# Recurrence products in column groups: the diagonal and four-block levels of a hybrid decoder trunk

## The chip, the cores and the metric

One core of a Trainium2 chip runs the whole kernel. The metric is the device time of one execution in microseconds (us), the median of several runs; a run that is profiled gives a trace as well. The engines are named as the profile names them: PE is TensorE (PEld its weight loads), DVE is VectorE, ACT is ScalarE, POOL is GpSimd, SP is SyncE, which issues the DMAs here.

## The reference

Two layers of a decoder trunk on 256 tokens of width 2048. In each layer a shared input projection feeds attention and, beside it, a gated linear recurrence of 8 heads (HGRN2) with 128 key and 128 value columns a head. Then come an output projection, a gated feed-forward part, and a gated input embedding. The change is in the recurrence alone:

```python
def hgrn2_chunkwise(q, k, v, log_f):
    ...
    def step(state, inp):
        q_, k_, v_, g_ = inp
        b = jnp.cumsum(g_, axis=2)
        diff = b[:, :, :, None, :] - b[:, :, None, :, :]
        decay = jnp.exp(jnp.where(causal[None, None, :, :, None], diff, MASK_VALUE))
        a = jnp.einsum('bhtk,bhsk,bhtsk->bhts', q_, k_, decay)
        o = jnp.einsum('bhts,bhsv->bhtv', a, v_) + \
            jnp.einsum('bhtk,bhkv->bhtv', q_ * jnp.exp(b), state)
```

So the score of a query token t against an earlier token s is a sum over the 128 key columns of q, k and the product of the forget gates between s and t.

## The kernel before

**Projections.** Nearly all of the time goes to large projections. Weights come by DMA in pieces of 256 rows and 512 columns (512 KB), 10 buffers (`wr`). ACT makes a rounded copy of each (`wh`, L305) and DVE the remainder (`wl`, L315), 7 buffers each. `strip` (L330, L331, L333) multiplies a piece by the two 128-token halves: three matmuls of 512 columns for each half and 128 rows, twelve a piece. After each piece `tick()` advances the work that runs beside the projections: generators and delayed functions. These emit their instructions between the projection's.

**Order.** The kernel is written with a tile framework. It finds the dependencies, and its scheduler lays out the order of each engine's instructions when the program is built; on the chip each engine keeps that order. `behind("pe")` holds an instruction behind the projection matmul emitted last. Accesses to one bank of PSUM (where TensorE writes its results) are kept apart: a read of a bank by DVE or ACT and a write to it by TensorE do not overlap. The small products share four banks (`bank()`, tag `ms`).

**The recurrence.** `Rec` handles four heads at once, and there are two groups a layer, so four `Rec` in all. Each runs beside the projections of its own gates (`done_f`, `done_q`, `done_i`, `done_g`). It holds q, k and the gates transposed (128 key columns in the partitions, tokens along the free axis) and fills the score tile `s.at` (source token s in the partitions, target t along the free axis, two halves of 128 tokens, four heads). It does so level by level, from small blocks of tokens to large ones:

- diagonal (`levels`, L1046): a token with itself and with its neighbour. For each half and head one product of k's 128 tokens (stationary) with `s.qd` (128 plain columns and 64 odd ones that carry one gate). DVE takes the diagonal by a multiplication with the identity (L1049) and the neighbours by a masked copy (L1051).
- four-block levels for blocks of 2 and of 8 tokens (`four`, L1009): one product for each half and head of k's 128 tokens with 192 columns of `s.qf`, then three masked copies (L1018) for every two heads. Between them `up`, `prepare` and `up_four` (L977 to L1038) multiply the gates into q, k and f on DVE and build the next `s.qf` (ACT L994, DVE L995 and L997).
- levels of 32 and 64 (L1075): only the blocks needed, 32 or 64 stationary columns, each block's result in its own partitions, copied by ACT (L1077).
- then the block between the two halves (L1082) and the products with v (L1101, L1102).

In the diagonal and four-block levels all 128 source tokens are multiplied with all columns, and only blocks within 32 tokens of the diagonal are kept. `s.at` is written whole by L1049, which puts zeros outside the diagonal. Each of these levels takes eight products, two to a bank, four banks.

Of the kernel before, what the change touches and what calls it, by code (L numbers as in the profile page):

```python
# [8 lines left out]
F32 = mybir.dt.float32  # L9
F32R = mybir.dt.float32r  # L10
I32 = mybir.dt.int32
AF = mybir.ActivationFunctionType
ALU = mybir.AluOpType
AX = mybir.AxisListType

P = 128
SEQ = 256
NT = 2
D = 2048
# [28 lines left out]
def decoder(ctx: ExitStack, tc: tile.TileContext, x, p, positions, w_in, attn_sinks,  # L48
# [9 lines left out]
    sp = ctx.enter_context(tc.tile_pool(name="sp", bufs=1))  # L58
# [6 lines left out]
    V, S, G, T = nc.vector, nc.scalar, nc.gpsimd, nc.tensor  # L65
# [41 lines left out]
    def bank(shape=(P, W)):  # L107
        return pms.tile(list(shape), F32, tag="ms", name="ms")
# [29 lines left out]
    ident = cp.tile([P, P], F32, name="ident")  # L138
# [22 lines left out]
    at = 0  # L161
    for g in (pre_ffn_gain, ple_gain, attn_out_gain, hgrn_out_gain):
        n = DEPTH * g.shape[1] // P
# [429 lines left out]
    m_one = cp.tile([P, 64], F32, name="m_one")  # L593
    m_four = cp.tile([P, 2, 192], F32, name="m_four")
# [155 lines left out]
    for l in range(DEPTH):  # L750
# [45 lines left out]
        def done_q(half):  # L796
            qT[half] = sp.tile([P, 4, SEQ], F32, tag="AB"[half], name="qT")

            def done(t, ps):
                tb = tables(t)  # L800
                o = nat()
                ov = o.rearrange("p (g two j d) -> p g j two d", j=4, g=2, two=2)
                rotate(ps, tb, 0, 8, ov[:, :, :, 0], ov[:, :, :, 1])
                start(attend(half, t, o))
            return done
# [107 lines left out]
        class Rec:  # L913


            def __init__(s, grp):
                s.grp = grp
                s.has_v = set()
                s.f = sp.tile([P, 4, SEQ], F32, tag="A", name="f")
                s.k = sp.tile([P, 4, SEQ], F32, tag="B", name="k")  # L920
                s.q = sp.tile([P, 4, SEQ], F32, tag="C", name="q")
                s.at = sp.tile([P, NT, 4, P], F32, tag="at", name="at")
                s.ax = sp.tile([P, 4, P], F32, tag="ax", name="ax")

            def done_f(s, t, ps):
                z = nat()
                S.activation(z, ps, AF.Copy, scale=rx(t)[:, 0:1])


                def turn():  # L930
                    pt = bank((P, 4, P))
                    for b in range(4):
                        T.transpose(pt[:, b], z[:, b * P:(b + 1) * P], ident)
                    cols = slice(t * P, (t + 1) * P)
                    S.activation(s.f[:, :, cols], pt, AF.Sigmoid)
                    S.activation(s.k[:, :, cols], pt, AF.Sigmoid, scale=-1.0)
                    for h in range(4):
                        c = s.grp * 4 + h
                        V.tensor_scalar(s.f[:, h, cols], s.f[:, h, cols], omlb[:, l, c:c + 1],
                                        lb[:, l, c:c + 1], op0=ALU.mult, op1=ALU.add)  # L940
                        V.tensor_scalar(s.k[:, h, cols], s.k[:, h, cols], omlb[:, l, c:c + 1],
                                        None, op0=ALU.mult)
                later(5, turn)

            def done_q(s, t, ps):
                sg = nat()
                S.activation(sg, ps, AF.Sigmoid, scale=rx(t)[:, 0:1])
                V.scalar_tensor_tensor(sg, ps, rx(t)[:, 0:1], sg, op0=ALU.mult, op1=ALU.mult)

                if t == 0:  # L950
                    s.qd = sp.tile([P, 4, NT, P + 64], F32, tag="D", name="qd")

                def turn():
                    pt = bank((P, 4, P))
                    for b in range(4):
                        T.transpose(pt[:, b], sg[:, b * P:(b + 1) * P], ident)
                    raw = s.qd[:, :, t, 0:P]
                    cols = slice(t * P, (t + 1) * P)
                    S.copy(raw, pt)

                    def odd(a):
                        return a.rearrange("p h (b two) -> p h b two", two=2)[:, :, :, 1]
                    V.tensor_tensor(s.qd[:, :, t, P:P + 64], odd(raw), odd(s.f[:, :, cols]),
                                    op=ALU.mult)
                    V.tensor_tensor(s.q[:, :, cols], raw, s.f[:, :, cols], op=ALU.mult)
                    if t == 1:
                        start(s.levels())
                later(3 - t, turn)
# [30 lines left out]

            def four(s, k):  # L1000

                for t in range(NT):
                    for h0 in (0, 2):
                        pl = bank((P, 2, 192))
                        for g in range(2):
                            h = h0 + g
                            c = h * 64 + t * 32
                            with behind("pe"):
                                T.matmul(pl[:, g].rearrange("p (b six k) -> p b six k", six=6, k=k),  # L1009
                                         s.k[:, h, t * P:(t + 1) * P],  # L1010
                                         s.qf[:, :, c:c + 32].rearrange("p v (b k) -> p b v k", k=k),
                                         start=True, stop=True)
                        at = s.at[:, t, h0:h0 + 2].rearrange("p g (b m) -> p g b m", m=4 * k)
                        pv = pl.rearrange("p g (b m) -> p g b m", m=6 * k)
                        mv = m_four[:, (2, 8).index(k)].rearrange("p (b m) -> p b m", m=6 * k)
                        for v0, n in ((0, 3), (3, 2), (5, 1)):
                            cols = slice(v0 * k, (v0 + n) * k)
                            V.copy_predicated(  # L1018
                                at[:, :, :, (4 - n) * k:4 * k],
                                mv[:, :, cols].bitcast(I32).unsqueeze(1)  # L1020
                                .to_broadcast([P, 2, 32 // k, n * k]),
                                pv[:, :, :, cols])

            def up_four(s, k):
                qv, kv, fv, qf = s.views(k)
# [13 lines left out]

            def levels(s):  # L1040
                yield
                for t in range(NT):
                    for h0 in (0, 2):
                        pd = bank((P, 2, P + 64))
                        for h in range(2):
                            T.matmul(pd[:, h], s.k[:, h0 + h, t * P:(t + 1) * P],  # L1046
                                     s.qd[:, h0 + h, t], start=True, stop=True)
                        at = s.at[:, t, h0:h0 + 2]
                        V.tensor_tensor(at, pd[:, :, 0:P],  # L1049
                                        ident.unsqueeze(1).to_broadcast([P, 2, P]), op=ALU.mult)  # L1050
                        V.copy_predicated(  # L1051
                            at.rearrange("p h (b two) -> p h b two", two=2)[:, :, :, 1],
                            m_one.bitcast(I32).unsqueeze(1).to_broadcast([P, 2, 64]),
                            pd[:, :, P:P + 64])
                s.up(1)
                s.prepare(2)
                yield
                yield
                yield
                s.four(2)  # L1060
                s.up_four(2)
                s.prepare(8)
                yield
                yield
                s.four(8)
                s.up_four(8)
                yield
                for k in (32, 64):
                    pl = bank((P, NT, 4, k))
                    for s0 in range(0, P, 2 * k):  # L1070
                        rows = slice(s0, s0 + k)
                        for t in range(NT):
                            for h in range(4):
                                c = t * P + s0
                                T.matmul(pl[rows, t, h], s.k[:, h, c:c + k],  # L1075
                                         s.q[:, h, c + k:c + 2 * k], start=True, stop=True)
                        S.copy(s.at[rows, :, :, s0 + k:s0 + 2 * k], pl[rows])  # L1077
                    s.up(k)
                    yield
                px = bank((P, 4, P))  # L1080
                for h in range(4):
                    T.matmul(px[:, h], s.k[:, h, 0:P], s.q[:, h, P:2 * P], start=True, stop=True)  # L1082
                S.copy(s.ax, px)
                yield
                for t in range(NT):
                    while t not in s.has_v:
                        yield
                    s.out(t)
# [119 lines left out]
        for gi, glen in enumerate(FF_GROUPS):  # L1208
# [3 lines left out]
            while len(hidden) < want:  # L1212
                n = len(hidden)
# [121 lines left out]
```

## Time and profile before

| | |
|---|---|
| median of 3 runs | 2378.17 us |
| lowest and highest | 2377.51, 2379.47 us |
| the profiled execution | 2380.66 us |
| its span, first to last instruction | 2378.9 us |
| granted TensorE clock | 0.998 |

A row of the groups gives line, engine, operation, tiles (out<-in), for TensorE the weights' size, the shapes, the count, then after the bar the busy time in us and the mean ns of one, and the idle time before them. A row of the timeline gives start and length in us, then the same, with the count of instructions merged into it and, in brackets, how long the engine stood idle before and what ended that. Matmuls overlap in a pipeline, so the length of one is more than its share of the time; the distance between starts is the share.

### The profile page before, as it was taken

Reading aid. Unit: us, or ns where it says so; the run is one execution under the profiler, and the core shown is the slowest. Engines: PE = TensorE matmul, PEld = TensorE weight load, DVE = VectorE, ACT = ScalarE, POOL = GpSimd, SP = SyncE. Lnnn points to the kernel's source line nnn. Section 1 sums busy time; section 2 is a strip of 40 time slices with the busy share of each in tenths; the row PEclk is TensorE's granted clock in tenths of the full one; section 3 lists DMA queues with packets and bytes.
Section 4 is the critical chain, followed back from the end, with each engine's and each line's share of the span. In section 5 each row is a group of like instructions: output and inputs, shape, how many; then the busy total and the mean of one; then the engine's idle time right before and its main releaser. Section 6 shows DMA issues by size and latency. Waiting matters only on the chain.

```text
span 2378.9 us, 31721 instructions
## 1 busy us (share of the span) xinstructions
PE 2358.3 (99%) x10951; PEld 1950.6 (82%) x10951; DVE 2026.5 (85%) x2703; ACT 1398.0 (59%) x2000; POOL 106.6 (4%) x213
## 2 busy tenths in 40 slices
PE   9999999999999999999999999999999999999999
PEld 7888887887888888888788888878878888888887
DVE  7687987999999899888777879779999989998885
ACT  6565466556556555657556554665566565565564
POOL 3100001000000000001010000010000000000010
PEclk9999999999999999999999999999999999999999
DMA  8666467657566664766776663675765575667753
GB/s 290 216 187 203 151 199 250 223 199 244 181 226 219 241 230 166 272 220 203 227 222 207 184 209 132 226 257 180 241 219 193 206 254 198 230 209 251 243 169 133
DMA packets 301666, 506.05 MB, mean 213 GB/s; under 512 B 23712, under 2 KB 69696, under 8 KB 301504
## 3 DMA queue, kind: packets, MB, share of 16 engines
q1 hardware_dynamic: 301200, 503.93, 63.6%
q8 instruction: 86, 1.41, 0.2%
q14 instruction: 76, 0.62, 0.1%
q10 hardware_dynamic: 240, 0.07, 0.0%
q0 software_dynamic: 64, 0.02, 0.0%
HBM read 474.57 MB, written 29.36 MB: 212 GB/s over the span
## 4 chain that ended last, share of the span: by engine, by line
PE 92%; DVE 4%; issue 1%; DMA 1%; ACT 1%; POOL 1%; SPq 0%; DVEq 0%; ACTq 0%; POOLq 0%
PE acc L331 9%; PE acc L330 9%; PE acc L333 9%; PE accc L418 5%; PE accc L421 5%; PE accc L422 5%; PE acca L422 4%; PE acce L422 4%; PE acce L418 4%; PE acca L418 4%; PE acca L421 4%; PE acce L421 4%; PE accd L422 3%; PE accd L418 3%; PE accd L421 3%; PE ms L418 3%
## 5 line engine op out<-in xcount | busy, mean ns | idle before, releaser
L305 ACT CAST wh<-wr 128x1024 fp32r<-128x1024 f32 x980 | 1006.0, 1051 | 722.9 <-DVE wr L434 209.3
L315 DVE TENSOR_TENSOR wl<-wr,wh 128x1024 fp32r<-128x1024 f32 x980 | 1163.0, 1217 | 212.7 <-ACT wh L305 204.9
L330 PE MATMUL acc<-wh,ck 128*128 128x512 f32 x1056 | 417.5, 396 | 0.8 <-ACT ck L203 0.8
L331 PE MATMUL acc<-wh,ck 128*128 128x512 f32 x1056 | 413.4, 392 | 0.0
L333 PE MATMUL acc<-wl,ck 128*128 128x512 f32 x1056 | 412.2, 391 | 0.8 <-DVE wl L315 0.8
L434 DVE TENSOR_TENSOR wr<-wr 128x1024 f32<-128x1024 f32 (+1 forms) x240 | 243.8, 1038 | 0.8
L333 PEld LDWEIGHTS acc<-wl,ck 128*128 128x128 f32 x1056 | 198.7, 188 | 43.0 <-DVE wl L315 1.7
L331 PEld LDWEIGHTS acc<-wh,ck 128*128 128x128 f32 x1056 | 198.9, 188 | 40.3 <-DVE ck L204 0.4
L330 PEld LDWEIGHTS acc<-wh,ck 128*128 128x128 f32 x1056 | 198.5, 188 | 40.6 <-ACT ck L203 1.0
L418 PE MATMUL acca<-wh,ck 128*128 128x512 f32 x468 | 182.6, 390 | 3.1 <-ACT wh L305 3.1
L422 PE MATMUL acca<-wl,ck 128*128 128x512 f32 x468 | 182.3, 390 | 1.1 <-DVE wl L315 1.1
L418 PE MATMUL acce<-wh,ck 128*128 128x512 f32 x468 | 182.7, 390 | 0.4 <-ACT wh L305 0.4
L422 PE MATMUL acce<-wl,ck 128*128 128x512 f32 x468 | 182.3, 390 | 0.3 <-DVE wl L315 0.2
L421 PE MATMUL acce<-wh,ck 128*128 128x512 f32 x468 | 182.1, 389 | 0.0
L421 PE MATMUL acca<-wh,ck 128*128 128x512 f32 x468 | 182.1, 389 | 0.0
L422 PE MATMUL accd<-wl,ck 128*128 128x512 f32 x368 | 144.7, 393 | 0.0
L418 PE MATMUL accd<-wh,ck 128*128 128x512 f32 x368 | 143.7, 390 | 0.0
L421 PE MATMUL accd<-wh,ck 128*128 128x512 f32 x368 | 143.2, 389 | 0.0
L421 PE MATMUL accc<-wh,ck 128*128 128x512 f32 x368 | 143.2, 389 | 0.0
L422 PE MATMUL accc<-wl,ck 128*128 128x512 f32 x368 | 143.2, 389 | 0.0
L418 PE MATMUL accc<-wh,ck 128*128 128x512 f32 x368 | 143.1, 389 | 0.0
L418 PEld LDWEIGHTS acca<-wh,ck 128*128 128x128 f32 x468 | 87.8, 188 | 22.9 <-ACT wh L305 4.8
(277 smaller groups left out, 3362.2 us busy)
## 6 DMA issues: line engine op xcount, KB each, us to landing
wr<-in_w_in_dram SPq DMA_DIRECT2D x176, 512.0 KB, 4.9
wr<-in_w_ffn_gate_dram SPq DMA_DIRECT2D x176, 512.0 KB, 6.0
wr<-in_w_ffn_up_dram SPq DMA_DIRECT2D x176, 512.0 KB, 6.1
wr<-in_w_ffn_down_dram SPq DMA_DIRECT2D x176, 512.0 KB, 7.4
wr<-in_w_out_dram SPq DMA_DIRECT2D x64, 512.0 KB, 4.9
wr<-in_w_ple_gate_dram SPq DMA_DIRECT2D x64, 512.0 KB, 5.5
turn<-nat SPq DMA_DIRECT2D x86, 256.0 KB, 2.6
nat<-turn SPq DMA_DIRECT2D x344, 64.0 KB, 3.6
```

The source lines that it names most:

```text
L305: marks["hi"] = S.copy(hi, raw)
L315: marks["lo"] = V.tensor_tensor(lo, raw, hi.bitcast(F32), op=ALU.subtract)
L330: T.matmul(ps[t], xh, hi[:, k], start=first, stop=False)
L331: T.matmul(ps[t], xl, hi[:, k], start=False, stop=False)
L333: marks[t, c] = marks["pe"] = T.matmul(ps[t], xh, lo[:, k], start=False, stop=last)
L418: T.matmul(ps, xh, hi[:, k], start=id(ps) not in opened, stop=False, skip_group_check=True)
L421: T.matmul(ps, xl, hi[:, k], start=False, stop=False, skip_group_check=True)
L422: marks["pe"] = T.matmul(ps, xh, lo[:, k], start=False, stop=k == ks[-1], skip_group_check=True)
L434: V.tensor_tensor(dst, p, q, op=ALU.subtract)
```

## The change

The score tile gets zeros from a memset when a `Rec` is set up. In the diagonal and the four-block levels each product of 128 source tokens with 192 columns becomes four products of 32 source tokens with the 48 columns that belong to the same 32 target tokens, and each result goes to the 32 partitions of its tokens. These are the four column groups of the array: the partitions that a result goes to are set by the stationary columns that made it. All 32 products of a level go into one bank. DVE then works on 32 partitions at a time, all halves and heads in one instruction (`diagonal` gives the 32 x 32 blocks of the score tile). `s.qd` is laid out in groups of 32 plain and 16 odd columns. In the levels of 32 and 64 the loops are exchanged: all products first, going from one block of source tokens to the next within each head, and then the copies.

```diff
                 s.ax = sp.tile([P, 4, P], F32, tag="ax", name="ax")
+                G.memset(s.at, 0.0)
+
+            def diagonal(s, j):
+
+                rows = slice(32 * j, 32 * j + 32)
+                return rows, s.at[rows].rearrange("p t h m -> p (t h) m")[:, :, rows]
...
-                    s.qd = sp.tile([P, 4, NT, P + 64], F32, tag="D", name="qd")
+                    s.qd = sp.tile([P, 4, NT, 4, 48], F32, tag="D", name="qd")
...
             def four(s, k):
 
+                pl = bank((P, NT, 4, 48))
                 for t in range(NT):
-                    for h0 in (0, 2):
-                        pl = bank((P, 2, 192))
-                        for g in range(2):
-                            h = h0 + g
-                            c = h * 64 + t * 32
+                    for h in range(4):
+                        for j in range(4):
+                            rows = slice(32 * j, 32 * j + 32)
+                            c = h * 64 + t * 32 + 8 * j
                             with behind("pe"):
-                                T.matmul(pl[:, g].rearrange("p (b six k) -> p b six k", six=6, k=k),
-                                         s.k[:, h, t * P:(t + 1) * P],
-                                         s.qf[:, :, c:c + 32].rearrange("p v (b k) -> p b v k", k=k),
+                                T.matmul(pl[rows, t, h].rearrange("p (b six k) -> p b six k", six=6, k=k),
+                                         s.k[:, h, t * P + 32 * j:t * P + 32 * j + 32],
+                                         s.qf[:, :, c:c + 8].rearrange("p v (b k) -> p b v k", k=k),
                                          start=True, stop=True)
...
+                for j in range(4):
+                    rows, at = s.diagonal(j)
+                    at = at.rearrange("p g (b m) -> p g b m", m=4 * k)
+                    pv = pl[rows].rearrange("p t h (b m) -> p (t h) b m", m=6 * k)
...
+                    for v0, n in ((0, 3), (3, 2), (5, 1)):
+                        cols = slice(v0 * k, (v0 + n) * k)
+                        V.copy_predicated(
+                            at[:, :, :, (4 - n) * k:4 * k],
...
             def levels(s):
                 yield
+                pd = bank((P, NT, 4, 48))
                 for t in range(NT):
...
+                    for h in range(4):
+                        for j in range(4):
+                            c = t * P + 32 * j
+                            T.matmul(pd[32 * j:32 * j + 32, t, h], s.k[:, h, c:c + 32],
+                                     s.qd[:, h, t, j], start=True, stop=True)
+                for j in range(4):
+                    rows, at = s.diagonal(j)
+                    pv = pd[rows].rearrange("p t h m -> p (t h) m")
+                    V.tensor_tensor(at, pv[:, :, 0:32], ident[rows, rows].unsqueeze(1)
+                                    .to_broadcast([32, 8, 32]), op=ALU.mult)
+                    V.copy_predicated(
...
                 for k in (32, 64):
                     pl = bank((P, NT, 4, k))
+                    for t in range(NT):
+                        for h in range(4):
+                            for s0 in range(0, P, 2 * k):
+                                c = t * P + s0
+                                T.matmul(pl[s0:s0 + k, t, h], s.k[:, h, c:c + k],
+                                         s.q[:, h, c + k:c + 2 * k], start=True, stop=True)
                     for s0 in range(0, P, 2 * k):
                         rows = slice(s0, s0 + k)
-                        for t in range(NT):
-                            for h in range(4):
-                                c = t * P + s0
-                                T.matmul(pl[rows, t, h], s.k[:, h, c:c + k],
-                                         s.q[:, h, c + k:c + 2 * k], start=True, stop=True)
                         S.copy(s.at[rows, :, :, s0 + k:s0 + 2 * k], pl[rows])
```

More of the change, by code (lines that the diff above doesn't have):

```diff
@@ L956, in turn, with groups, odd @@
                         T.transpose(pt[:, b], sg[:, b * P:(b + 1) * P], ident)
-                    raw = s.qd[:, :, t, 0:P]
-                    cols = slice(t * P, (t + 1) * P)
[L959 to L965, printed above, removed]
+                    raw = s.qd[:, :, t, :, 0:32]
+                    def groups(a):
+                        return a.rearrange("p h (j m) -> p h j m", j=4)
+                    def odd(a):
+                        return a.rearrange("p h j (b two) -> p h j b two", two=2)[:, :, :, :, 1]
+                    cols = slice(t * P, (t + 1) * P)
+                    S.copy(raw, groups(pt))
+                    f = groups(s.f[:, :, cols])
+                    V.tensor_tensor(s.qd[:, :, t, :, 32:48], odd(raw), odd(f), op=ALU.mult)
+                    V.tensor_tensor(groups(s.q[:, :, cols]), raw, f, op=ALU.mult)
                     if t == 1:
@@ L1012, in four @@
                                          start=True, stop=True)
[L1013 to L1022, printed above, removed]
+                for j in range(4):
+                    rows, at = s.diagonal(j)
+                    at = at.rearrange("p g (b m) -> p g b m", m=4 * k)
+                    pv = pl[rows].rearrange("p t h (b m) -> p (t h) b m", m=6 * k)
+                    mv = m_four[rows, (2, 8).index(k), 48 * j:48 * j + 48].rearrange(
+                        "p (b m) -> p b m", m=6 * k)
+                    for v0, n in ((0, 3), (3, 2), (5, 1)):
+                        cols = slice(v0 * k, (v0 + n) * k)
+                        V.copy_predicated(
+                            at[:, :, :, (4 - n) * k:4 * k],
+                            mv[:, :, cols].bitcast(I32).unsqueeze(1)
+                            .to_broadcast([32, 8, 8 // k, n * k]),
+                            pv[:, :, :, cols])
@@ L1041, in levels @@
                 yield
+                pd = bank((P, NT, 4, 48))
                 for t in range(NT):
[L1043 to L1054, printed above, removed]
+                    for h in range(4):
[9 more added lines that the diff above has]
+                    V.copy_predicated(
+                        at.rearrange("p g (b two) -> p g b two", two=2)[:, :, :, 1],
+                        m_one[rows, 16 * j:16 * j + 16].bitcast(I32).unsqueeze(1)
+                        .to_broadcast([32, 8, 16]), pv[:, :, 32:48])
                 s.up(1)
```

## The prediction

> **What bounds the kernel now.** I read the page first: span, busy shares, and the chain that ended last.
>
> ```profile
> span 2378.9 us, 31721 instructions
> ...
> PE 2358.3 (99%) x10951; PEld 1950.6 (82%) x10951; DVE 2026.5 (85%) x2703; ACT 1398.0 (59%) x2000; POOL 106.6 (4%) x213
> ...
> PE 92%; DVE 4%; issue 1%; DMA 1%; ACT 1%; POOL 1%; SPq 0%; DVEq 0%; ACTq 0%; POOLq 0%
> ```
>
> TensorE is busy 99% of the span and carries 92% of the chain. So whatever shortens its instruction stream shortens the kernel, as long as nothing it waits for comes later than it does today. DVE, at 85%, is the only engine near enough to matter. The second view is the list of TensorE's instructions by line and shape, for the lines that the diff rewrites:
>
> ```profile
> L1009 PE MATMUL ms<-qf,k 128*128 128x192 f32 x128 | 22.5, 328 | 0.0
> ...
> L1046 PE MATMUL ms<-qd,k 128*128 128x192 f32 x64 | 11.0, 326 | 0.0
> ...
> L1075 PE MATMUL ms<-q,k 128*32 128x32 f32 x128 | 5.5, 197 | 0.0
> ```
>
> A product shows as two records: 64 four-block products give 128 rows, 32 diagonal products give 64. The busy time of the two lines, 33.5 us, is 1.4% of the span, and that is the whole pool the change can draw on, apart from the 5.5 us of L1075's smaller level. L1075 already uses 32 columns of the array, so it is the nearest row to what comes.
>
> **What a level costs today.** The timeline, TensorE alone, around one diagonal level, one four-block level, and the level with blocks of 32:
>
> ```profile
> 160.60 0.39 PE L333 MATMUL acc<-wl,ck 128*128 128x512 f32 x1
> 160.83 2.76 PE L1046 MATMUL ms<-qd,k 128*128 128x192 f32 x16
> 163.29 0.53 PE L330 MATMUL acc<-wh,ck 128*128 128x512 f32 x1
> 163.66 0.39 PE L331 MATMUL acc<-wh,ck 128*128 128x512 f32 x1
> ```
>
> ```profile
> 170.03 0.39 PE L333 MATMUL acc<-wl,ck 128*128 128x512 f32 x1
> 170.26 2.83 PE L1009 MATMUL ms<-qf,k 128*128 128x192 f32 x16
> 172.78 0.53 PE L330 MATMUL acc<-wh,ck 128*128 128x512 f32 x1
> 173.15 0.40 PE L331 MATMUL acc<-wh,ck 128*128 128x512 f32 x1
> ```
>
> ```profile
> 188.71 0.39 PE L331 MATMUL acc<-wh,ck 128*128 128x512 f32 x1
> 189.02 0.69 PE L1075 MATMUL ms<-q,k 128*32 128x32 f32 x16
> 189.65 0.50 PE L333 MATMUL acc<-wl,ck 128*128 128x512 f32 x1
> 189.98 0.39 PE L330 MATMUL acc<-wh,ck 128*128 128x512 f32 x1
> 190.21 0.40 PE L331 MATMUL acc<-wh,ck 128*128 128x512 f32 x1
> 190.54 0.69 PE L1075 MATMUL ms<-q,k 128*32 128x32 f32 x16
> 191.16 0.50 PE L333 MATMUL acc<-wl,ck 128*128 128x512 f32 x1
> 191.50 0.39 PE L330 MATMUL acc<-wh,ck 128*128 128x512 f32 x1
> ```
>
> Durations overlap, so I work with starts. One projection matmul follows another after 0.23 us (189.98 to 190.21). The net cost of an excursion is the time from the start of the last projection matmul before it to the start of the second one after it, less 2 x 0.23. Diagonal: 163.66 - 160.60 - 0.46 = 2.60 us. Four-block: 173.15 - 170.03 - 0.46 = 2.66 us. There are four diagonal levels and eight four-block levels (two layers, two head groups): 4 x 2.60 + 8 x 2.66 = 31.7 us. The level of 32 makes two excursions, 189.98 - 188.71 - 0.46 = 0.81 and 191.50 - 190.21 - 0.46 = 0.83, so 1.64 us, and 6.6 us in the four groups.
>
> Now a record's own price. Sixteen records of 192 columns take 2.83 us from first start to last end, so (2.83 - 0.33) / 15 = 167 ns from one to the next; sixteen of 32 columns (0.69 - 0.20) / 15 = 33 ns. That is 134 ns for 160 columns, 0.84 ns each, and so 33 + 16 x 0.84 = 46 ns for 48 columns, an estimate between those two rows. The 32-wide excursion also has a fixed part, 0.81 - 16 x 0.033 = 0.28 us, and 0.30 for the second: I take 0.29 us for going to a narrow shape and back. The wide excursions show none (2.60 / 16 = 163 ns a record).
>
> **Do different groups run at the same time?** This decides everything. No row of column groups used alternately exists: L1075 stays in one group for sixteen records. The nearest is the attention scores, which alternate between two row groups:
>
> ```profile
> 73.99 1.16 PE L839 MATMUL ms<-kv,qT 64*128 64x128 f32 x16 [0.19 <-ACT qT L811]
> ```
>
> ```profile
> 73.99 0.38 PE L839 MATMUL ms<-kv,qT 64*128 64x128 f32 x2 [0.19 <-ACT qT L811]
> ```
>
> ```profile
> 107.35 1.89 PE L897 MATMUL ms<-kv,nat 128*128 128x64 f32 x16
> ```
>
> Sixteen records of 128 columns take 1.16 us, at most 73 ns each, where the line through my two rows gives 33 + 96 x 0.84 = 114 ns. The second row is the first two of them: both lie within 0.38 us, so they start together. So row groups overlap, and their weight loads too: L897 streams only 64 columns (60 ns by the line) and yet takes up to 118 ns a record, which is the price of loading 128 weight columns, and the scores load 128 columns each and beat it. Whether column groups do the same is my inference from row groups, not a reading.
>
> **The change part by part.** Each 192-column product becomes four of 48 columns into four groups: 16 records become 64 a level. If four groups run at once, the 64 are 16 rounds of 46 ns, 0.74 us, plus 0.29 us: 1.03 us a level, 12.4 us in twelve levels, 19.3 us less than 31.7. Bounds: 64 x 46 ns = 2.94 + 0.29 = 3.23 us (no overlap at all), so from -19.3 to +7.1 us; I take the overlapping end because the row that alternates groups shows it. The level of 32 now does both column groups in one excursion: 16 rounds x 33 ns + 0.29 = 0.82 us instead of 1.64, 3.3 us in four groups (without overlap 32 x 33 ns + 0.29 = 1.35 us, 1.2 us saved). The level of 64 keeps its order.
>
> Vector work keeps its count (two instructions four times on a diagonal, three four times on a four-block level) and its elements per partition (256, 128, and 192, 128, 64); each covers 32 partitions instead of 128. I take no change. The memset of the score tile is new, on POOL:
>
> ```profile
> L614 POOL MEMSET m_neg<- 128x128 f32 x1 | 0.2, 213 | 0.0
> ```
>
> Eight times the elements is at most 8 x 0.213 = 1.7 us, four times. POOL is 4% busy, and the tile is first written by DVE strips later; behind the memset on POOL stand the rotations and the powers of the norms. I take nothing; with no cover at all it would be 6.8 us.
>
> The real charge is DVE. Each level ends in vector work that prepares the next one, and TensorE's order, fixed when the kernel is built, puts the next level just where that work is done:
>
> ```profile
> 169.55 0.41 DVE L997 TENSOR_TENSOR qf<-qf,f 128x256 f32<-128x256 f32 x1
> ...
> 170.08 2.70 PEld L1009 LDWEIGHTS ms<-qf,k 128*128 128x128 f32 x16
> ```
>
> ```profile
> 180.25 0.42 DVE L997 TENSOR_TENSOR qf<-qf,f 128x256 f32<-128x256 f32 x1
> ...
> 180.88 2.69 PEld L1009 LDWEIGHTS ms<-qf,k 128*128 128x128 f32 x16
> ```
>
> ```profile
> 261.68 0.42 DVE L997 TENSOR_TENSOR qf<-qf,f 128x256 f32<-128x256 f32 x1
> ...
> 264.69 0.41 PEld L1009 LDWEIGHTS ms<-qf,k 128*128 128x128 f32 x2
> ```
>
> ```profile
> 160.00:190.00 30.00, 30.00 (x160) 25.93 (x159) 29.89 (x67) 12.39 (x15) 0.00 (x0) 1.00 0.50 143
> ```
>
> DVE ends the operand at 169.96 and 180.67, and TensorE starts loading 0.12 and 0.21 us later; in the third pair it has 2.6 us in hand. In the window of 160 to 190 us (columns: length, then PE, PEld, DVE, ACT, POOL) DVE is busy 29.89 of 30.00 us. So a TensorE that reaches the next level 1.6 us sooner finds its operand not ready, and the projection matmuls queued behind the waiting product stand still with it, unless the rebuilt order puts more of them in front. There is also one bank a level now instead of four, so DVE starts on it when all 64 records are done, not a quarter of them. The loss lies between nothing and all of the 19.3 us. By the tight pairs it would be most of it, by the loose pair and a new order none; I take half, 9.7 us. The Trainium skill, "TensorEngine Tiling (Array Packing)", section "PSUM Bottleneck", warns of just this: packing speeds up the products but not the emptying of PSUM, which may become the limit. By that rule the full 19.3 us goes and 3.3 us stay; by the row at 264.69 all 22.6 us stay; the trace has both kinds.
>
> Sum: 19.3 + 3.3 - 9.7 = 12.9 us. The profiled execution has a span of 2378.9 us and took 2380.66 us, 1.8 us outside the span; the median of the three runs is 2378.17 us, so I subtract there: 2378.2 - 12.9 = 2365.3, say 2365 us. With no loss 2355.6, with all of it 2374.9.
>
> **The rivals.**
> One at a time at the gate. Records of different column groups may still start no closer than L1075's 33 ns, because their weight loads or their starts take turns. For: that is the closest steady spacing of narrow records in this trace, and a quarter of L897's 118 ns is 30 ns for 32 weight columns. Against: the two score records that start together. A level is 64 x 33 ns + 0.29 = 2.40 us, 31.7 - 28.8 = 2.9 us saved, with 1.2 us from the level of 32: 4.1 us, 2374 us. The page named above (section "Instruction Overhead") puts some 60 cycles on every matmul; an estimate by it is 25 ns a record and a gain of 11 us before any wait, and no row here shows such a floor across groups.
>
> Groups take turns altogether. The products of one column group finish streaming before the next group's begin. The place is TensorE in all twelve levels, the price 3.23 us a level; the change loses as soon as a record costs over (2.64 - 0.29) / 64 = 37 ns. 12 x 3.23 - 31.7 = 7.1 us more, less 1.2 us: 2384 us. For: all groups share the same 128 rows, unlike the scores. Against: nothing but those scores.
>
> Loads are not hidden. If a narrow load waits until the product before it is done, a record is 46 + 30 = 76 ns, a level 5.15 us, 30 us more in twelve, some 2.7 us more in the level of 32: 2411 us. Against it: L1075's 33 ns holds load and product together. The Trainium skill, "TensorE: Matmul & The Clock Gate", Part 3, "The mechanism", says that a load overlaps running matmuls only where the row group differs, which here it never does; L1075 and L897, at full rate in one row group, disagree.
>
> The change does not do what it says: the build scatters the 64 records between projection matmuls, and each extra excursion costs 0.29 us. Some 78 extra ones would eat the 22.6 us; that lands between 2365 and 2380.
>
> **How the numbers follow.** 0.2% is 4.8 us, about what a measurement of this kernel can tell from no change. Forecast 0.53 (0.47 faster by more than that, 0.06 within it, where nearly all is lost to DVE). One at a time 0.23: its 4.1 us lies at the bound, 0.10 faster, 0.13 same. Turns 0.16: 5.9 us, 0.11 slower, 0.05 same. Loads not hidden 0.04, slower. Scattered 0.04, half same, half slower. Faster 0.57, same 0.26, slower 0.17. The range goes from the forecast with no loss, 2355.6, to groups taking turns, 2384.1: 2356 to 2384. The forecast's own range is 2356 to 2375.
>
> **What would show it.** In the changed trace, the diagonal should be 64 records in one row of the timeline, of about 1 us; 2.3 us there means the gate, 3.1 us turns, near 5 us exposed loads. Between the records of one round, starts should lie a few ns apart. The lost half should show as idle time of TensorE before the four-block products, ended by DVE's L997 or its counterpart. DVE's total should stay near 2026 us, and the 32-wide level should be one excursion of 0.8 us. I am wrong if TensorE shows no such waits and the time is under 2356, or if a level takes over 2.6 us.

## The result, and the profile after

The changed kernel takes 2388.44 us (median of 5 runs, 2385.95 to 2390.74) against 2378.17 us: a ratio of 1.0042, with a 95% interval of 1.0031 to 1.0054. It is slower by 10 us, outside the predicted range. The page of the profiled execution, which took 2388.44 us: span, busy times, and the chain that ended last by engine.

```profile
span 2386.7 us, 32869 instructions
...
PE 2343.5 (98%) x11527; PEld 1928.2 (81%) x11527; DVE 2042.3 (86%) x2703; ACT 1397.2 (59%) x2000; POOL 112.1 (5%) x217
...
PE 85%; DVE 10%; issue 1%; DMA 1%; POOL 1%; ACT 1%; SPq 0%; DVEq 0%; ACTq 0%; POOLq 0%
```

TensorE's busy time fell by 14.8 us, yet it idles 2386.7 - 2343.5 = 43.2 us where it idled 2378.9 - 2358.3 = 20.6. DVE has the same 2703 instructions and 15.8 us more busy time, and its share of the chain went from 4% to 10%. The next fence is the timeline, TensorE alone: a diagonal level, and then, from another window, a four-block level.

```profile
255.34 0.39 PE L333 MATMUL acc<-wl,ck 128*128 128x512 f32 x1
255.66 0.89 PE L1059 MATMUL ms<-qd,k 128*32 128x48 f32 x64
256.47 0.50 PE L330 MATMUL acc<-wh,ck 128*128 128x512 f32 x1
256.81 0.40 PE L331 MATMUL acc<-wh,ck 128*128 128x512 f32 x1
```

```profile
168.24 0.39 PE L333 MATMUL acc<-wl,ck 128*128 128x512 f32 x1
169.42 0.90 PE L1018 MATMUL ms<-qf,k 128*32 128x48 f32 x64 [0.80 <-DVE qf L1006]
170.26 0.50 PE L330 MATMUL acc<-wh,ck 128*128 128x512 f32 x1
```

By the prediction's own rule the diagonal costs 256.81 - 255.34 - 0.46 = 1.01 us net, where 1.03 was forecast and 2.60 stood before. The array does what was hoped. But the four-block products, as short as that, stand still before they start, for DVE's L1006. TensorE's waits by line, the four longest in total (us in total, times, longest):

```profile
PE ms L1018 <- DVE qf L1006: 9.8, 6, 2.6
PE ms L225 <- DVE ho L1134: 4.1, 2, 2.1
PE acc L330 <- ACT wh L305: 3.3, 2, 1.7
PE ms L1089 <- DVE k L1048: 3.3, 3, 1.4
```

In the kernel before, TensorE has no wait for DVE in the levels.

Why is DVE late? Its instructions are no longer than before, as the mean of the widest copy shows, before and after (the last number ahead of the second bar, in ns):

```profile
L1018 DVE COPY_PREDICATED at<-m_four,ms 128x192 f32<-128x192 int32 x32 | 13.0, 406 | 1.0 <-PE ms L1009 0.9
```

```profile
L1030 DVE COPY_PREDICATED at<-m_four,ms 32x192 f32<-32x192 int32 x32 | 13.0, 407 | 0.6
```

The timeline of DVE alone in a four-block level shows it (start, length, so the sum is the end):

```profile
171.38 0.43 DVE L1030 COPY_PREDICATED at<-m_four,ms 32x192 f32<-32x192 int32 x1
171.69 0.65 DVE L1046 TENSOR_TENSOR k<-k,f 128x512 f32<-128x512 f32 x1
172.28 0.28 DVE L1030 COPY_PREDICATED at<-m_four,ms 32x128 f32<-32x128 int32 x1
172.48 0.63 DVE L1047 TENSOR_TENSOR f<-f 128x256 f32<-128x256 f32 x1
173.03 0.73 DVE L1030 COPY_PREDICATED at<-m_four,ms 32x64 f32<-32x64 int32 x2
173.79 0.69 DVE L1048 TENSOR_TENSOR k<-k,f 128x512 f32<-128x512 f32 x1
174.51 0.29 DVE L1030 COPY_PREDICATED at<-m_four,ms 32x128 f32<-32x128 int32 x1
174.83 0.42 DVE L1050 TENSOR_TENSOR f<-f 128x128 f32<-128x128 f32 x1
```

The first four rows and the first copy of the fifth work on partitions that start at 0, and each starts before the one ahead has ended: 171.69 against 171.38 + 0.43 = 171.81. From the second copy of the fifth row on, the copies start at partition 32 and the gate work at 0, and the overlap is gone: 173.79 + 0.69 = 174.48, next start 174.51; 174.51 + 0.29 = 174.80, next start 174.83. In the whole trace 216 neighbouring pairs have a level's vector instruction in them. In 172 of these the second starts up to 60 ns after the first has ended, on average 27 ns (these are called held below); in the other 44 they overlap by 83 ns. In the kernel before, where every vector instruction starts at partition 0, two of 156 pairs have such a gap, and the usual pair looks like this (174.86 against 174.26 + 0.68 = 174.94):

```profile
174.26 0.68 DVE L1034 TENSOR_TENSOR k<-k,f 128x512 f32<-128x512 f32 x1
174.86 0.29 DVE L1018 COPY_PREDICATED at<-m_four,ms 128x64 f32<-128x64 int32 x1
```

### The profile page after: what moved, and what is told of

It reads as the page before. It is cut to its first block, busy times and chain, and to the rows that moved or that the text cites. A ratio compares the mean times of both kernels' runs of the same rounds, so it can differ in the third digit from the quotient of the medians.

```text
span 2386.7 us, 32869 instructions
## 1 busy us (share of the span) xinstructions
PE 2343.5 (98%) x11527; PEld 1928.2 (81%) x11527; DVE 2042.3 (86%) x2703; ACT 1397.2 (59%) x2000; POOL 112.1 (5%) x217
## 4 chain that ended last, share of the span: by engine, by line
PE 85%; DVE 10%; issue 1%; DMA 1%; POOL 1%; ACT 1%; SPq 0%; DVEq 0%; ACTq 0%; POOLq 0%
PE acc L333 8%; PE acc L331 8%; PE acc L330 8%; PE accc L422 5%; PE accc L421 5%; PE accc L418 5%; PE acca L422 4%; PE acca L421 4%; PE acca L418 4%; PE acce L422 4%; PE acce L418 4%; PE acce L421 4%; PE accd L422 3%; PE accd L421 3%; PE accd L418 3%; DVE wl L315 3%
## 5 line engine op out<-in xcount | busy, mean ns | idle before, releaser
L315 DVE TENSOR_TENSOR wl<-wr,wh 128x1024 fp32r<-128x1024 f32 x980 | 1161.0, 1219 | 205.4 <-ACT wh L305 197.7
L330 PE MATMUL acc<-wh,ck 128*128 128x512 f32 x1056 | 417.9, 396 | 3.8 <-ACT wh L305 3.3
L330 PEld LDWEIGHTS acc<-wh,ck 128*128 128x128 f32 x1056 | 199.1, 189 | 45.2 <-ACT wh L305 3.8
```

The lines of the kernel that those rows point to most:

```text
L315: marks["lo"] = V.tensor_tensor(lo, raw, hi.bitcast(F32), op=ALU.subtract)
L330: T.matmul(ps[t], xh, hi[:, k], start=first, stop=False)
```

## The experiments

Two theories. **Handover**: a vector instruction that starts at another group of 32 partitions than the one before waits for that one's end, and this alone makes DVE late. **Early arrival**, which was the prediction's own charge: TensorE is done sooner and meets DVE's ordinary work unfinished. Each ratio below is to runs of the kernel before made beside that run; their median was 2378.66 us for e1 to e4 and 2379.47 us for e5 to e7.

**One start partition (e1).** All of the change, with the vector instructions of the levels on partitions 0 to 31.

```diff
-                return rows, s.at[rows].rearrange("p t h m -> p (t h) m")[:, :, rows]
+                return slice(0, 32), s.at[0:32].rearrange("p t h m -> p (t h) m")[:, :, rows]
```

> The changed kernel with every vector instruction of the diagonal and four-block levels on partitions 0 to 31: same count, same elements per partition, and the order of DVE and of TensorE unchanged instruction by instruction. Left out: the results of source tokens 32 to 127 of each 128 (their blocks of the score tile stay zero or get the first quadrant's numbers). Handover theory: in the changed trace a vector instruction that starts at another group of 32 partitions than the one before starts 13 to 31 ns after that one has ended, where otherwise two overlap by some 70 to 90 ns; with one start partition the overlap returns, the roughly 5 us that a DVE chain of diagonal and two four-block levels gained per head group vanish, and the time is 2358 to 2370 us. Early-arrival theory: TensorE waits because its levels are shorter and DVE's own work has its old length; then nothing changes and the time stays 2384 to 2391 us.

Measured: 2365.15 us, ratio to the kernel before 0.9948 [0.9933, 0.9963], 23.3 us under the changed kernel with the same instructions in the same order. The page, and DVE's timeline at the same level:

```profile
span 2362.2 us, 32875 instructions
...
PE 2335.0 (99%) x11527; PEld 1923.7 (81%) x11527; DVE 2023.9 (86%) x2703; ACT 1397.5 (59%) x2000; POOL 114.2 (5%) x217
```

```profile
171.16 0.66 DVE L1048 TENSOR_TENSOR k<-k,f 128x512 f32<-128x512 f32 x1
171.75 0.28 DVE L1030 COPY_PREDICATED at<-m_four,ms 32x128 f32<-32x128 int32 x1
171.95 0.40 DVE L1050 TENSOR_TENSOR f<-f 128x128 f32<-128x128 f32 x1
```

The overlap is back (171.75 against 171.16 + 0.66 = 171.82), in 212 of the 216 pairs, by 95 ns on average. A handover so costs 27 + 95 = 122 ns, and 172 of them 21 us of DVE. The 23.3 us of the whole kernel are of that size but are not the same sum: between the two profiled spans (24.5 us), TensorE's idle time differs by 43.2 - 27.2 = 16.0 us, and its 11527 records are busy 8.5 us longer in the changed kernel, at a mean granted clock of 0.997 against 1.000 (last section). No four-block product waits for DVE in this trace. Early arrival falls here: TensorE's levels are as short and in the same order, and the wait is gone.

**Handovers without the change (e2, e3).** The kernel before, with the four banks of a level taken out on four different groups of 32 partitions, or all on the first.

```diff
-                        at = s.at[:, t, h0:h0 + 2].rearrange("p g (b m) -> p g b m", m=4 * k)
-                        pv = pl.rearrange("p g (b m) -> p g b m", m=6 * k)
+                        i = 2 * t + h0 // 2
+                        rows = slice(32 * i, 32 * i + 32)
+                        at = s.at[rows, t, h0:h0 + 2].rearrange("p g (b m) -> p g b m", m=4 * k)
+                        pv = pl[rows].rearrange("p g (b m) -> p g b m", m=6 * k)
```

The second run has `rows = slice(0, 32)`; the diagonal is cut in the same way.

> The kernel before, with its 192-column products and its four banks a level, but each vector instruction that takes a bank out works on 32 partitions only, bank 0 on partitions 0 to 31, bank 1 on 32 to 63 and so on: same count and the same elements per partition as before. The score tile is cleared by a memset as in the change. Left out: the other 96 rows of each bank. Nothing of TensorE's gain is in it. Handover theory: the vector chain of a head group grows by some 3 to 5 us, TensorE waits for most of it, and the time is 2385 to 2396 us, with gaps of 13 to 31 ns before such instructions. Early-arrival theory: TensorE is not early, so the time stays 2375 to 2381 us.

> The same with all of these instructions on partitions 0 to 31; the order of DVE and of TensorE is instruction by instruction that of the run before it. Left out: rows 32 to 127 of each bank. Both theories: 2375 to 2381 us, the time of the kernel before. If it is slow as well, 32 partitions or the memset cost the time, and not the change of the start partition.

Measured: 2397.46 us, ratio 1.0079 [1.0064, 1.0094], and 2379.33 us, ratio 1.0002 [0.9992, 1.0011]. A stretch of DVE's copies in one four-block level, first with four start partitions, then with one:

```profile
174.32 3.00 DVE L1021 COPY_PREDICATED at<-m_four,ms 32x128 f32<-32x128 int32 x8
```

```profile
171.59 2.08 DVE L1021 COPY_PREDICATED at<-m_four,ms 32x192 f32<-32x192 int32 x9
```

Eight copies take 3.00 us, nine take 2.08. In the first trace 133 of 156 pairs are held, by 30 ns on average, and in the second the pairs overlap by 100 ns: 133 x 130 ns = 17.3 us, and the times differ by 18.1 us. Here too the wait is the four-block products' for DVE (9.6 us in six waits in the first run, none in the second). The first run came out a little over its range. The control also clears the memset (it is in both runs) and the 32 partitions as such.

**Whole-width vector work (e4).** The change, with DVE on all 128 partitions and a narrow tile between.

```diff
+                s.ad = sp.tile([P, NT * 4, 32], F32, tag="ad", name="ad")
...
-                for j in range(4):
-                    rows, at = s.diagonal(j)
...
+                V.tensor_tensor(s.ad, pv[:, :, 0:32], c_id.unsqueeze(1)
+                                .to_broadcast([P, 8, 32]), op=ALU.mult)
...
+            def spread(s):
+                for j in range(4):
+                    rows, at = s.diagonal(j)
+                    S.copy(at, s.ad[rows])
```

> The column-group products of the change, but DVE takes each bank out in instructions of all 128 partitions into a narrow tile of 32 columns a head and half, with the masks of one 32-token block for all partitions, and ACT spreads this tile into the diagonal blocks of the score tile in four copies a head group. A quarter of the vector instructions in these levels (2 on a diagonal, 3 on a four-block level), and no change of start partition on DVE. All of the computation is there. Handover theory: TensorE keeps its 22.6 us and the waits go: 2352 to 2362 us, with DVE's busy time some 20 us under the 2026.5 us of before. Early-arrival theory: the gate work between the levels still ends when it did, so TensorE's waits before the four-block products stay and the time is 2365 to 2380 us.

Measured: 2357.63 us, ratio 0.9918 [0.9903, 0.9933], the fastest of all: 21 us under the kernel before.

```profile
span 2355.0 us, 32828 instructions
...
PE 2333.8 (99%) x11527; PEld 1924.1 (82%) x11527; DVE 2003.8 (85%) x2607; ACT 1406.8 (60%) x2028; POOL 113.5 (5%) x217
```

TensorE idles 21.2 us, about what it did before the change (20.6), so nearly all of its gain reaches the end. DVE is 22.7 us below the kernel before: its 24 small copies and 8 for the diagonal of a head group became 6 and 2, and the four spreading copies went to ACT.

**The exchanged loops alone (e5).** The kernel before with this edit of the change.

```diff
-                    for s0 in range(0, P, 2 * k):
-                        rows = slice(s0, s0 + k)
-                        for t in range(NT):
-                            for h in range(4):
+                    for t in range(NT):
+                        for h in range(4):
+                            for s0 in range(0, P, 2 * k):
```

> The kernel before with one part of the change: in the levels of 32 and 64 all products first, alternating between the blocks of source tokens within each head, then the copies. All of the computation is there. Overlapping groups: the level of 32 becomes one excursion of 0.8 us instead of two of 0.8, 0.8 us in each of four head groups, and the time is 2373 to 2377 us. Groups that take turns: 1.35 us instead of 1.64, and 2376 to 2379 us.

Measured: 2376.63 us, ratio 0.9985 [0.9975, 0.9994]. TensorE in the level of 32:

```profile
190.03 0.39 PE L331 MATMUL acc<-wh,ck 128*128 128x512 f32 x1
190.35 0.70 PE L1074 MATMUL ms<-q,k 128*32 128x32 f32 x32
190.97 0.50 PE L333 MATMUL acc<-wl,ck 128*128 128x512 f32 x1
191.31 0.39 PE L330 MATMUL acc<-wh,ck 128*128 128x512 f32 x1
```

32 records now take what 16 took: 191.31 - 190.03 - 0.46 = 0.82 us, as forecast. The ratio comes to 3.6 us of gain (3.3 forecast), with an interval of 1.4 to 6 us. The ranges of the two theories met at 2376 to 2377 us, so it is the row that decides, for overlapping groups.

**One column group after the other (e6).** The version of e4, with `for j in range(4)` as the outermost loop of the products instead of the innermost.

> The compact version, with the products of a level ordered group by group: all sixteen records of column group 0, then those of group 1, and so on, instead of changing the group with every product. Same instructions, same vector work, and all of the computation. If the gain of TensorE comes from column groups at work at the same time, a level takes 64 records at 46 ns and 0.29 us, 3.2 us instead of 1.03, and the time rises from 2357.6 by up to 26 us, to 2375 to 2386 us. If narrow products are merely cheap one by one, a level keeps about 1 us and the time stays 2354 to 2361 us.

Measured: 2376.28 us, ratio 0.9989 [0.9979, 0.9998], 18.7 us over e4. A diagonal level of e6, and the same level of e4:

```profile
253.70 0.39 PE L333 MATMUL acc<-wl,ck 128*128 128x512 f32 x1
254.01 2.49 PE L1078 MATMUL ms<-qd,k 128*32 128x48 f32 x64
256.43 0.50 PE L330 MATMUL acc<-wh,ck 128*128 128x512 f32 x1
256.77 0.39 PE L331 MATMUL acc<-wh,ck 128*128 128x512 f32 x1
```

```profile
247.46 0.39 PE L333 MATMUL acc<-wl,ck 128*128 128x512 f32 x1
247.77 0.89 PE L1078 MATMUL ms<-qd,k 128*32 128x48 f32 x64
248.59 0.50 PE L330 MATMUL acc<-wh,ck 128*128 128x512 f32 x1
248.93 0.40 PE L331 MATMUL acc<-wh,ck 128*128 128x512 f32 x1
```

The same 64 records take 256.77 - 253.70 - 0.46 = 2.61 us instead of 248.93 - 247.46 - 0.46 = 1.01, 1.60 us more, and 12 levels x 1.60 = 19 us, about the difference in time. So the gain is column groups at work at once, and the order of the products is what lets them be.

**Fewer handovers by order (e7).** The changed kernel, each vector instruction of a level tied behind the one before it, quadrant by quadrant, and the gate work behind them.

```diff
+                        with chained(s):
+                            s.last = V.copy_predicated(
...
+                with chained(s):
+                    s.up_four(2)
+                    s.prepare(8)
```

(`chained` issues what it holds behind `s.last`.)

> The changed kernel with its vector instructions of a level issued quadrant by quadrant next to each other, the gate work of the level behind them and not between. Same instructions, all of the computation; on a four-block level about 5 to 7 changes of the start partition instead of about 20, on the diagonal 8 instead of 13. Handover theory: each change costs about 0.1 us, so the four-block levels lose 1.3 us of their 2 and the time falls from 2388 to 2372 to 2382 us, between the changed kernel and the run with one start partition (2365). Early-arrival theory: no such fall, 2384 us or more, since the gate work comes later behind the copies.

Measured: 2389.64 us, ratio 1.0043 [1.0026, 1.006]: no gain. This is what early arrival said, but the trace shows that the edit did not do what it was for. Of 186 pairs 149 still do not overlap: the build put splits of weights (L315) between the copies, and three copies in one quadrant write the same columns one after another, so that each waits for the last (gaps of 32 to 35 ns). TensorE's longest waits are now:

```profile
PE acce L418 <- DVE nat L1145: 5.5, 2, 3.1
PE ms L1025 <- ACT wh L305: 5.0, 2, 2.5
PE ms L1025 <- DVE qf L1013: 4.7, 4, 1.5
```

The four-block products wait as long as in the changed kernel (5.0 + 4.7 = 9.7 us against 9.8), and waits for L1145 are new; that the gate work behind the copies made them is likely but not shown. The run tells neither theory from the other, and whether a true reduction of handovers on the way to e1 pays in proportion was not tried.

## Why the prediction was wrong

**What held.** Column groups overlap as the row groups of the scores did: 1.01 us a diagonal level where 1.03 was forecast, 0.82 us for the level of 32 where 0.82 was. "One at a time at the gate", "turns" and "loads not hidden" are out: 64 records start within 0.89 us, each with its own weight load. The Trainium skill, "TensorE: Matmul & The Clock Gate", Part 3, "The mechanism", ties overlapping loads to different row groups; here the row group never differs, and yet 64 records with their loads take 0.89 us in e4 and 2.49 us group by group in e6, so they overlap all the same. (Of the two rows that the prediction set against that page, only L1075 bears on it; L897, at 118 ns a record, is not at the 60 ns of its 64 columns.) The prices of 46 ns and 2.94 us for records in turn were too high: e6 gives (2.61 - 0.29) / 64 = 36 ns.

**What failed.** The step is the term for vector work, which was put at nothing because count and elements per partition stay: "each covers 32 partitions instead of 128. I take no change." Count and length did stay (L1030 407 ns, L1018 of before 406), but not the spacing: 172 handovers at 122 ns, 21 us of DVE, many of them where it was already busy 29.89 of 30.00 us. The prediction priced a vector instruction by its duration alone, where the distance from start to start was the share of the path; for TensorE it had made just that distinction. With no row of before showing a vector instruction on another group of 32 partitions, it should have been bounded from both sides. The Trainium skill, "VectorE: DVE Perf Modes", section "Two Vector instructions with no wait between them", states it: an instruction whose input or output starts in another 32-partition quadrant than the last one's in the same memory is held until all earlier vector instructions have finished. The traces agree, with 0.12 us for each. With that term the sum would have set 22.6 us of gain against 21 us more of DVE: about no change, and still not the 10 us of loss. The prediction's cap on the loss fell with the term. It let DVE take back 19.3 us at most, what TensorE gains in the levels that wait; TensorE's idle time grew by 43.2 - 20.6 = 22.6 us, and of the 23.3 us that its busy time falls in e1 the changed kernel shows 14.8.

**The loss to DVE.** I took 9.7 us for TensorE arriving early. The place was right, the cause was not: at one start partition no four-block product waits. Of TensorE's gain e1 still loses some: its busy time is 23.3 us under that of before and its span 16.7, so 6.6 us went into new idle time, on other lines, among them L330 for ACT's `wh` (3.3 us in two waits). Its time of 2365 us is the predicted one by accident. e4 has another order and nearly none of this; which of its differences removes it, fewer vector instructions or the order, was not separated.

**The emptying of PSUM.** It did become the limit, but not by its volume: e1 empties the same number of elements per partition and gains 13.5 us. The Trainium skill, "TensorEngine Tiling (Array Packing)", section "PSUM Bottleneck", warns of such a limit; the traces agree that it is there, and put it down to the spacing.

**Scattered products.** This rival was partly so: in two of the head groups the diagonal's 64 records came as 32 and 32, with a net 0.67 and 0.68 us in one of them, 0.3 us more than one piece. POOL's memset took 0.96 us each time, and the control shows no cost.

## What to carry to other kernels

Cut a product into column groups and alternate the groups from one product to the next; group by group, nearly all of the gain was gone. Then look at who empties the bank: keep each vector instruction on all partitions, even if it needs a narrow tile and copies on another engine, because here vector instructions that changed their first partition lost their overlap. Price a vector instruction by the distance between starts, with its neighbours, not by its length.

## What the runs showed of the hardware

That handover costs about 0.12 us on DVE was not expected, nor that a short instruction pays about as much as a long one. In the timelines above, behind the 0.69 us multiplication L1048 the next start moves from 0.07 us before its end (e1) to 0.03 us after it, and behind the 0.29 us copy from 0.08 before to 0.03 after.

The changed kernel also ran at a lower clock for short times. Two waits of the four-block products, equally long:

```profile
274.00 1.06 PE L1018 MATMUL ms<-qf,k 128*32 128x48 f32 x64 [2.57 <-DVE qf L1006]
```

```profile
1460.09 0.89 PE L1018 MATMUL ms<-qf,k 128*32 128x48 f32 x64 [2.57 <-DVE qf L1006]
```

These are the windows around them, and the first window in e1 (length, then PE, PEld, DVE, ACT, POOL, PEclk, DMA share, GB/s):

```profile
250.00:280.00 30.00, 27.43 (x327) 21.90 (x325) 29.04 (x58) 12.42 (x15) 0.00 (x0) 0.94 0.43 147
1440.00:1470.00 30.00, 25.77 (x327) 20.27 (x326) 28.84 (x60) 12.07 (x15) 0.00 (x0) 1.00 0.37 119
```

```profile
250.00:280.00 30.00, 30.00 (x354) 24.09 (x353) 29.39 (x70) 14.40 (x18) 0.00 (x0) 1.00 0.36 110
```

The clock is 0.94 around the first wait and 1.00 around the second and in e1. So a wait of this length can go with a lower clock and need not; what decides it is not shown. Three more windows of the changed kernel are at 0.94 (1150 to 1180, 1410 to 1440 and 1480 to 1510 us); the first of them is at 0.94 in the kernel before too. The four together make 4 x 30 x 0.06 = 7 us, an estimate, of the 8.5 us by which TensorE's busy time is above that of e1.
